# Bringing V back from DRAM by row groups of 32 partitions instead of by key blocks

## The chip, the cores and the metric

The kernel runs on one core of one Trainium2 chip. The metric is the device time of one execution in microseconds. The kernel before takes 347.27 us (median of 3 runs, 345.57 to 350.7). The profile that this document reads is one further execution with a time of its own, 347.75 us, whose span from the first to the last instruction is 346.0 us. Engines are named as the profile names them: PE is TensorE, PEld its weight loads, DVE is VectorE, ACT is ScalarE, POOL is GpSimd, SP is SyncE, which here issues nearly all the DMAs.

## The reference, cut to what matters

Two transformer mixers run one after the other on 256 positions of width 1024, each after an RMS norm whose scale, shift and gate come from a conditioning vector c:

```
cond = silu(c)
for i in range(2):
    shift, scale, gate = split(cond @ ada_w[i] + ada_b[i], 3)
    h = rms_norm(x, norm_g[i]) * (1 + scale) + shift
    y = nsa_mixer(h, ...) if i == 0 else moba_mixer(h, ...)
    x = x + gate * y
```

Both mixers project h by a matrix (`w_in`, to q, keys, values and a gate z), normalise and rotate q and k, attend with 16 heads that share 4 key/value heads of 64 channels, multiply by silu(z) and project back (`w_out`). At 256 positions the selection of blocks in both mixers keeps every block that a query may see. So layer 0 (NSA) adds up three attentions: over 15 compressed keys, over all earlier keys, and over a window, with two separate sets of keys and values (`ks, vs` and `kw, vw`). Its compressed keys come from blocks of 32 positions that go through a small network (`cmp_w1`, a GELU, `cmp_w2`). Layer 1 (MoBA) is one causal attention with one set of keys and values.

## The kernel before, in words

Positions lie in two tiles of 128 (m = 0, 1). Weights come from DRAM in pieces of 512 KB into five buffers named `raw` (`plan.tag("raw", ...)`, line 584; the first projection's pieces use twelve buffers `early`). ACT rounds a piece to `hi`, DVE takes the rest to `lo`, and the `raw` buffer is free again once DVE has read it; PE multiplies with `hi` and `lo` in three passes (`product`). Pieces of `cmp_w1` and of the conditioning matrix `ada_w` are multiplied by PE straight from `raw`, and free it when PE has read it.

**V's way through DRAM.** The products of weights and V work on a quarter of the PE array each: `values` (line 1032) multiplies 32 keys by 64 channels in row group a, the partitions 32a to 32a+31. Row group a needs, for every key block b of 32 keys, that block's V on its own partitions. V comes out of the projection with one position on each partition, so it goes through a DRAM scratch tensor, `VD`. `spread` (line 1129) writes V to `VD` in one DMA (`vd<-n_out` in the profile) and reads it back with eight: for each of the two key tiles kt and each of four key blocks b, one DMA brings the 32 rows of block b four times, once to each row group. `spread` is called once in each layer (lines 1244 and 1525). A row of V has 512 elements in layer 0 (two sets of values) and 256 in layer 1. In layer 0, key tile 0 lands in the tensor `X` (whose content is reloaded later) and key tile 1 in the buffer `vr`; in layer 1 both land in `vr`. In layer 0 the compression network stands at the same place of the program: `cmp_steps` (line 1267) has four steps, and step kq multiplies two pieces of `cmp_w1`, one for keys and one for values. Steps 0 and 1 use pieces loaded before the read-backs or beside them, steps 2 and 3 pieces that come after.

**What sets the order.** All code is recorded first. `Plan._order` then plays the recorded steps in a simple model of the engines: whenever an engine is free, it takes the step that can start first, and among equals the one with the lowest number in the table `TURNS` (2333 numbers, one for each step). Each engine executes its steps strictly in the order that results, and so does SP with the DMAs. In the model a DMA's data are seen `LANDED` = 700 ns after its last byte. No instruction's work depends on the model's times; they set the order alone.

Of the kernel before, what the change touches and what calls it, by code (L numbers as in the profile page):

```python
# [18 lines left out]
P = 128  # L19
# [19 lines left out]
BREATH = 3000.0  # L39
TURNS = [  # L40
# [116 lines left out]
ISSUE, FIRST_BYTE, RATE, LANDED = 450.0, 1500.0, 330.0, 700.0  # L157
# [12 lines left out]
class Plan:  # L170
# [101 lines left out]
    def record(self, engine, method, args, kw):  # L272
# [13 lines left out]
        if "dma" in method:  # L286
            op["bytes"] = self.bytes
        if engine == "T":
            op["mode"] = (aps[1].shape[0], aps[1].shape[-1]) if "tile_position" in kw else None
# [1315 lines left out]
```

## Time and profile before

| | |
|---|---|
| median of 3 runs | 347.27 us |
| profiled execution | 347.75 us, span 346.0 us |
| PE busy | 308.0 us, 89% of the span |
| DVE busy | 248.8 us, 72% |
| ACT busy | 198.6 us, 57% |
| POOL busy | 26.3 us, 8% |
| moved by DMA | 70.89 MB, 205 GB/s over the span |
| mean granted PE clock | 0.964 |

In the profile nearly all work carries line 509, the line at which `issue` hands out recorded steps, so tiles are told apart by name. `raw<-in_nsa_cmp_w_dram` is a load of a piece of `cmp_w1`; `vr<-vd` and `X<-vd` are the read-backs of V; `vd<-n_out` is the write of V to DRAM. In a row of the timeline stand the start, the duration, the engine, the operation, the tile written and the tiles read, a count, and in brackets how long the engine stood idle before it and who released it. In a row of the windows stand, for a stretch of the span, its length, the busy time of each engine, the PE clock granted on average, the mean busy share of the 16 DMA engines, and what they moved. A row that SP has is the issuing of a DMA, not its transfer.

### The profile page before, as it was taken

Reading aid. Unit: us, or ns where it says so; the run is one execution under the profiler, and the core shown is the slowest. Engines: PE = TensorE matmul, PEld = TensorE weight load, DVE = VectorE, ACT = ScalarE, POOL = GpSimd, SP = SyncE. Lnnn points to the kernel's source line nnn. Section 1 sums busy time; section 2 is a strip of 40 time slices with the busy share of each in tenths; the row PEclk is TensorE's granted clock in tenths of the full one; section 3 lists DMA queues with packets and bytes.
Section 4 is the critical chain, followed back from the end, with each engine's and each line's share of the span. In section 5 each row is a group of like instructions: output and inputs, shape, how many; then the busy total and the mean of one; then the engine's idle time right before and its main releaser. Section 6 shows DMA issues by size and latency. Waiting matters only on the chain.

```text
span 346.0 us, 7930 instructions
## 1 busy us (share of the span) xinstructions
PE 308.0 (89%) x3147; PEld 246.5 (71%) x3147; DVE 248.8 (72%) x521; ACT 198.6 (57%) x466; POOL 26.3 (8%) x98
## 2 busy tenths in 40 slices
PE   3999999998058799999999999999993799999995
PEld 2866686886025587877678878866782699998874
DVE  3364363796309689887879497897592599999896
ACT  5444153833205487469578694587481389969430
POOL 5000007960000000000000000010000000000000
PEclk9999999999659989999999999999998799999999
DMA  8999995364759925966786617925439364255543
GB/s 249 333 359 357 364 359 164 96 177 139 192 162 312 303 71 184 300 196 221 270 265 227 236 61 221 309 82 160 127 129 294 113 185 121 73 182 178 163 142 121
DMA packets 46688, 70.89 MB, mean 205 GB/s; under 512 B 3914, under 2 KB 21945, under 8 KB 46652
## 3 DMA queue, kind: packets, MB, share of 16 engines
q1 hardware_dynamic: 46484, 70.34, 64.3%
q8 instruction: 24, 0.39, 0.5%
q14 instruction: 12, 0.10, 0.1%
q10 hardware_dynamic: 168, 0.06, 0.1%
HBM read 68.55 MB, written 1.84 MB: 203 GB/s over the span
## 4 chain that ended last, share of the span: by engine, by line
PE 63%; DVE 12%; DMA 11%; ACT 5%; issue 3%; ACTq 0%; DVEq 0%
PE ps L509 38%; PE acc L509 25%; DMA raw<-in_moba_w_in_dram 5%; DMA raw<-in_nsa_cmp_w_dram 4%; DVE lo L509 4%; DVE p L509 2%; ACT hi L509 2%; DMA raw<-in_nsa_w_in_dram 2%; DVE rs L509 2%; DVE n_out L509 1%; ACT p L509 1%; DVE n_in L509 1%; DVE ss L509 1%; ACT n_out L509 0%; ACT n_in L509 0%
## 5 line engine op out<-in xcount | busy, mean ns | idle before, releaser
L509 DVE TENSOR_TENSOR lo<-raw,hi 128x1024 fp32r<-128x1024 f32 (+1 forms) x50 | 58.9, 1188 | 20.1 <-ACT hi L509 20.0
L509 ACT CAST hi<-raw 128x1024 fp32r<-128x1024 f32 (+1 forms) x50 | 50.7, 1025 | 35.2 <-PE acc L509 13.0
L509 PE MATMUL acc<-hi,HT 128*128 128x512 f32 (+1 forms) x176 | 56.7, 395 | 8.2 <-ACT hi L509 8.2
L509 PE MATMUL acc<-HT,hi 128*128 128x256 f32 x256 | 49.6, 288 | 0.0
L509 ACT ACTIVATE p<-ps,tiny 128x128 f32<-128x128 f32 (+1 forms) x96 | 39.4, 425 | 14.6 <-DVE tiny L509 9.1
L509 PEld LDWEIGHTS acc<-hi,HT 128*128 128x128 f32 x176 | 32.7, 193 | 16.4 <-ACT hi L509 9.3
L509 PEld LDWEIGHTS acc<-HT,hi 128*128 128x128 f32 x256 | 40.0, 189 | 2.9 <-issue 2.5
L509 PE MATMUL acc<-HT,lo 128*128 128x256 f32 x128 | 35.8, 285 | 0.0
L509 PE MATMUL acc<-lo,HT 128*128 128x512 f32 (+1 forms) x88 | 33.8, 395 | 1.5 <-DVE lo L509 1.5
L509 PE MATMUL ps<-KTA,qg 128*128 128x256 f32 (+1 forms) x192 | 31.4, 297 | 3.3 <-ACT qg L509 2.0
L509 PEld LDWEIGHTS ps<-KTA,qg 128*128 128x128 f32 x192 | 26.9, 197 | 7.3 <-ACT qg L509 2.1
L509 DVE TENSOR_REDUCE tiny<-ps 128x2 f32<-128x512 f32 (+2 forms) x40 | 24.8, 630 | 9.7 <-PE ps L509 8.6
L509 PE MATMUL ps<-hi,HT 128*128 128x512 f32 (+1 forms) x96 | 27.1, 362 | 0.0
L509 PEld LDWEIGHTS acc<-HT,lo 128*128 128x128 f32 x128 | 23.9, 189 | 1.2 <-DVE lo L509 0.8
L509 PE MATMUL ps<-hi,qg 128*128 128x256 f32 (+1 forms) x96 | 22.9, 320 | 0.0
L509 PE MATMUL acc<-hi,qg 128*128 128x512 f32 x64 | 21.2, 400 | 0.9 <-DVE zT L509 0.9
L509 DVE STREAM_TRANSPOSE p<-p 128x1536 f32<-128x1536 f32 x12 | 21.2, 1770 | 1.0 <-ACT p L509 1.0
L509 ACT ACTIVATE p<-p,tiny 128x256 f32<-128x256 f32 x48 | 21.1, 501 | 1.3 <-DVE tiny L509 1.1
L509 PE MATMUL ps<-raw,p 128*64 128x256 f32 x64 | 10.4, 447 | 12.4 <-issue 7.9
L509 PEld LDWEIGHTS acc<-lo,HT 128*128 128x128 f32 x88 | 16.8, 193 | 6.0 <-DVE lo L509 3.4
L509 PEld LDWEIGHTS ps<-hi,HT 128*128 128x128 f32 x96 | 16.9, 188 | 4.7 <-issue 2.3
L509 ACT ACTIVATION_READ_ACCUMULATOR p<-ps,tiny 128x1 f32 x96 | 20.1, 209 | 0.0
(197 smaller groups left out, 565.0 us busy)
## 6 DMA issues: line engine op xcount, KB each, us to landing
raw<-in_ada_w_dram SPq DMA_DIRECT2D x32, 512.0 KB
raw<-in_moba_w_in_dram SPq DMA_DIRECT2D x20, 512.0 KB
early<-in_ada_w_dram SPq DMA_DIRECT2D x16, 512.0 KB
early<-in_nsa_w_in_dram SPq DMA_DIRECT2D x12, 512.0 KB
raw<-in_nsa_w_in_dram SPq DMA_DIRECT2D x12, 512.0 KB
raw<-in_nsa_cmp_w_dram SPq DMA_DIRECT2D x8, 512.0 KB
raw<-in_nsa_w_out_dram SPq DMA_DIRECT2D x8, 512.0 KB
raw<-in_moba_w_out_dram SPq DMA_DIRECT2D x8, 512.0 KB
```

The source lines that it names most:

```text
L509: getattr(self.engines[op["engine"]], method)(*[self._real(a) for a in args], **{k: self._real(a) for k, a in kw.items()})
```

## The change

The eight read-backs of a layer are cut the other way. One DMA now belongs to a row group a and a key tile: it writes the 32 partitions of that group, and each partition receives four rows of V, one from each key block, side by side. Bytes, rows and row lengths are the same as before: eight DMAs of 256 KB in layer 0 and eight of 128 KB in layer 1. What differs is the shape of each: before, the source was walked as 4 (the same block again) x 32 rows and the destination was 128 partitions with one row each; now the source is 32 x 4 rows and the destination 32 partitions with four rows each.

In the planner's model, a DMA that writes to DRAM is now seen 2500 ns after its last byte (`WRITTEN`), where it was 700 ns. The table `TURNS` is another one throughout.

```
+WRITTEN = 2500.0
 TURNS = [
-    43, 50, 44, 32, 67, 40, 45, 47, 48, 68, 2321, 2326, 51, 60, 2301, 92, 2330, 2329, 2331, 2332, 41, 81, 63, 54, 77,
...
+    53, 14, 13, 51, 47, 2296, 45, 54, 46, 15, 10, 12, 2292, 22, 2286, 2287, 2328, 2327, 2330, 2331, 69, 59, 60, 16, 31,
...
         if "dma" in method:
             op["bytes"] = self.bytes
+            op["landed"] = WRITTEN if str(args[0].space).endswith("DRAM") else LANDED
...
                 wire = max(wire, start + ISSUE + FIRST_BYTE) + op["bytes"] / RATE
-                seen = wire + LANDED
+                seen = wire + op["landed"]
...
         for kt, dst in enumerate(parts):
-            for b in range(4):
-                at = bass.AP(tensor=VD[l].tensor, offset=VD[l].offset + (kt * P + 32 * b) * n, ap=[[0, 4], [n, 32], [1, n]])
-                Q.dma_start(dst[:, b], at, touches=(dst[:, b], VD[l]))
+            for a in range(4):
+                to = dst[32 * a:32 * a + 32]
+                at = bass.AP(tensor=VD[l].tensor, offset=VD[l].offset + kt * P * n, ap=[[n, 32], [32 * n, 4], [1, n]])
+                Q.dma_start(to, at, touches=(to, VD[l]))
```

The new order is close to the old one on each engine except in the first projection, where PE takes the products of the pieces in another sequence. Three places matter below. The first is SP's queue in layer 0, from the last of the first six read-backs to the first piece of the next projection. Before:

```order
L509 DMA X_69<-vd0_131 128x1x512
L509 DMA raw_0_544<-in_nsa_cmp_w1_dram 128x4x256
L509 DMA vr_0_808<-vd0_131 128x1x512
L509 DMA raw_3_668<-in_nsa_cmp_w1_dram 128x4x256
L509 DMA raw_4_674<-in_nsa_cmp_w1_dram 128x4x256
L509 DMA raw_1_568<-in_nsa_cmp_w1_dram 128x4x256
L509 DMA raw_2_604<-in_nsa_w_in_dram 128x2x512
```

Now, where the first row stands for two read-backs:

```order
L511 DMA X_69<-vd0_131 32x4x512 x2
L511 DMA raw_0_571<-in_nsa_cmp_w1_dram 128x4x256
L511 DMA raw_3_686<-in_nsa_cmp_w1_dram 128x4x256
L511 DMA raw_4_704<-in_nsa_cmp_w1_dram 128x4x256
L511 DMA raw_1_587<-in_nsa_cmp_w1_dram 128x4x256
L511 DMA raw_2_627<-in_nsa_w_in_dram 128x2x512
```

Six read-backs stand ahead of the four pieces for steps 2 and 3 in both; a seventh stood between these pieces before and now comes later, after five more loads of the next stage, and the eighth comes later still.

The second place is PE's queue at step 2 of the compression. `ps<-identF,y` are the transposes that make the keys of layer 0 (four in a row), `acc<-..HT` the last products of the stage before, and `ps<-raw,p` the compression's products. Before:

```order
L509 MATMUL acc_0_283<-lo_0_228,HT_126 128x304
L509 MATMUL acc_0_283<-hi_3_322,HT_126 128x304
L509 MATMUL ps_2_182<-identF_71,y_0_146 128x128 x4
L509 MATMUL ps_3_203<-identF_71,y_1_346 128x128 x4
L509 MATMUL ps_5_230<-identF_71,y_0_146 128x128 x4
L509 MATMUL ps_1_177<-raw_0_544,p_1_742 64x256
L509 MATMUL ps_1_177<-raw_3_668,p_0_740 64x256
```

Now:

```order
L511 MATMUL acc_0_283<-lo_2_319,HT_126 128x304
L511 MATMUL acc_0_283<-hi_3_322,HT_126 128x304
L511 MATMUL ps_1_165<-identF_71,y_0_146 128x128 x4
L511 MATMUL ps_5_230<-identF_71,y_1_361 128x128 x4
L511 MATMUL ps_3_203<-raw_0_571,p_1_752 64x256
L511 MATMUL ps_3_203<-raw_3_686,p_0_747 64x256
```

The third group of transposes has moved from ahead of step 2 to behind it; the rest is as before, in other buffers.

The third place is SP's queue in layer 1, from the write of V on; `raw<-in_moba_w_in` are pieces of layer 1's projection. Before:

```order
L509 DMA vd1_132<-n_out_1_253 128x2x256
L509 DMA raw_3_668<-in_moba_w_in_dram 128x2x512
L509 DMA raw_0_544<-in_moba_w_in_dram 128x2x512
L509 DMA vr_0_808<-vd1_132 128x1x256 x8
L509 DMA raw_4_674<-in_moba_w_in_dram 128x2x512
```

Now:

```order
L511 DMA vd1_132<-n_out_1_253 128x2x256
L511 DMA raw_1_587<-in_moba_w_in_dram 128x2x512
L511 DMA raw_2_627<-in_moba_w_in_dram 128x2x512
L511 DMA vr_0_811<-vd1_132 32x4x256 x5
L511 DMA raw_0_571<-in_moba_w_in_dram 128x2x512
L511 DMA vr_0_811<-vd1_132 32x4x256
L511 DMA raw_1_587<-in_moba_w_in_dram 128x2x512
```

Five read-backs, not eight, now stand ahead of the next piece; one follows it, and two come after four more pieces.

226 rows, old and new, of the table TURNS are left out of this document.

## The prediction

> **What bounds the kernel now.** I read the page's slices first, then windows around the places where PE is not full, the chain that ended last, and SP's and PE's timelines there. In the page's 40 slices (8.65 us each) PE is full except at the start and the end and at two holes:
>
> ```profile
> PE   3999999998058799999999999999993799999995
> PEclk9999999999659989999999999999998799999999
> ```
>
> The holes are the slices from 86.5 us and from 259.5 us, and in both PEclk falls: the clock follows the idling. The chain names what ended them:
>
> ```profile
> 85.36 13.62 DMA raw<-in_nsa_cmp_w_dram
> 258.83 10.06 DMA raw<-in_moba_w_in_dram
> ```
>
> Both are waits for weight pieces, the first for the compression's, the second for layer 1's projection. The windows say what the DMA engines did meanwhile:
>
> ```profile
> core 0: us, PE busy (x) PEld busy (x) DVE busy (x) ACT busy (x) POOL busy (x), PEclk, DMA share, GB/s
> 74.00:83.00 9.00, 7.60 (x59) 6.67 (x58) 8.64 (x26) 0.61 (x2) 1.22 (x4) 1.00 0.29 107
> 104.00:110.00 6.00, 5.12 (x28) 3.20 (x24) 5.79 (x15) 3.10 (x4) 0.00 (x0) 1.00 0.99 346
> 247.00:252.00 5.00, 5.00 (x24) 4.08 (x23) 4.31 (x15) 2.37 (x5) 0.00 (x0) 1.00 0.85 255
> 252.00:259.00 7.00, 7.00 (x32) 5.77 (x31) 7.00 (x11) 5.88 (x7) 0.00 (x0) 1.00 0.28 95
> 123.00:260.00 137.00, 133.68 (x1647) 106.77 (x1647) 111.28 (x228) 97.45 (x254) 0.96 (x1) 1.00 0.59 190
> ```
>
> With weight pieces in flight (104 to 110 us) the engines are 99% busy and move 346 GB/s. While V comes back (74 to 83 and 252 to 259 us) 28 or 29% of them are busy and move 95 to 107 GB/s: between four and five of 16. Four is the outermost count of these transfers' source. Between the holes PE is busy for 133.68 of 137 us at full clock, so what is gained at the first hole stays gained: everything behind it follows PE.
>
> **First hole: 14.5 us if the read-backs use all engines.** SP's and PE's rows (a raw load's row covers the issue of the x pieces):
>
> ```profile
> 68.47 2.45 SPq L509 DMA_DIRECT2D raw<-in_nsa_cmp_w_dram  x2
> 71.43 0.64 SPq L509 DMA_DIRECT2D vr<-vd  x1
> 77.21 2.50 SPq L509 DMA_DIRECT2D X<-vd  x1
> 79.81 2.51 SPq L509 DMA_DIRECT2D raw<-in_nsa_cmp_w_dram  x1
> 85.36 7.94 SPq L509 DMA_DIRECT2D raw<-in_nsa_cmp_w_dram  x3
> 78.78 3.74 PE L509 MATMUL ps<-raw,p 128*64 128x256 f32 x32 [0.92 <-DVE p L509]
> 84.38 1.18 PE L509 MATMUL ps<-identF,y 128*128 128x128 f32 x8 [0.28 <-ACT y L509]
> 99.03 3.66 PE L509 MATMUL ps<-raw,p 128*64 128x256 f32 x14 [3.59 <-DMA raw<-in_nsa_cmp_w_dram]
> 103.20 1.95 PE L509 MATMUL ps<-raw,p 128*64 128x256 f32 x16
> ```
>
> Steps 0 and 1 of the compression run from 78.78 to 82.52 us; step 2 waits until 99.03 for its second piece, and step 3 ends at 103.20 + 1.95 = 105.15. The late read-backs take SP 2.5 us each to issue: 256 KB at 107 GB/s are 2.45 us, so SP is held to the four engines' pace, and the pieces behind it start late as well.
>
> Now the same with all engines. Up to 71.43 what differs is the order within the first projection (below) and one 48-column load that stands three rows later in SP's queue; PE multiplies three other pieces ahead of its use, so I cost it at nothing, or a microsecond if that cover is gone. The first read-back starts as before, and the engines are free of the two pieces ahead at about 74. Six read-backs are 1.57 MB: 4.5 us at 346 GB/s, to 78.5. Step 2's first piece (0.52 MB, 1.5 us) follows, to 80.0. Its second piece needs the buffer that step 0 frees, half way through PE's first row at 80.65. From issue to use I take 4.7 us, from a piece on full engines:
>
> ```profile
> 102.72 3.36 SPq L509 DMA_DIRECT2D raw<-in_nsa_w_in_dram  x3
> 107.43 1.05 ACT L509 CAST hi<-raw 128x1024 fp32r<-128x1024 f32 x1 [1.86 <-DMA raw<-in_nsa_w_in_dram]
> ```
>
> (102.72 to 107.43). That gives 85.4; step 3's last piece, whose buffer is free at 82.52, comes at 87.2. PE has transposed until 85.56. So step 2 runs to 87.5 (1.95 us at full clock), the two groups of transposes to 88.7, step 3 to 90.7. Against 105.15 this is 14.5 us, and DVE and ACT work that waited behind it moves along. What is late next is the projection's pieces. Their buffers are freed by steps 1 to 3, and DMA in the stage is the cap:
>
> ```profile
> 74.00:119.30 45.30, 28.88 (x176) 19.77 (x174) 25.87 (x66) 13.66 (x24) 1.22 (x4) 0.85 0.70 211
> ```
>
> 45.3 us at 211 GB/s are 9.56 MB. At 346 GB/s they take 27.6 us, to 101.6; the stage would end at 119.3 - 14.5 = 104.8. It fits, with 3.2 us to spare.
>
> **Do 32 partitions use all engines?** No read-back of that shape is in the trace. Small loads are:
>
> ```profile
> rot<-in_c_dram ACTq DMA_DIRECT2D x1, 4.0 KB
> y<-in_norm_g_dram ACTq DMA_DIRECT2D x1, 8.0 KB
> y<-in_ada_b_dram ACTq DMA_DIRECT2D x1, 24.0 KB
> y<-in_nsa_cmp_b_dram ACTq DMA_DIRECT2D x1, 2.0 KB
> y<-in_nsa_cmp_pe_dram ACTq DMA_DIRECT2D x1, 16.0 KB
> q10 hardware_dynamic: 168, 0.06, 0.1%
> ```
>
> In rows of 512 B these are 8, 16, 48, 4 and 32 rows, 108 packets. The queue shows 168, 60 more, which is 8 + 16 + 16 + 4 + 16: one more packet for each engine if a transfer uses the largest count up to 16 that divides its rows. The 32-row load then used 16; with 4 the sum would be 156. The Trainium skill, DMA: Bandwidth & Descriptors, section on why a DMA increments its semaphore by 16, states both this count and one completion write per engine.
>
> The rate of such a transfer is unknown. Upper bound: 346 GB/s. Lower, short of no change: half of it, 173. Against the change speaks the Trainium skill's SBUF page (SBUF — State Buffer), section Door 1, the DMA port swizzle: 32 neighbouring partitions reach 8 of 16 ports, measured at 189 GB/s against 328 for 128 partitions; no transfer here shows it, and its ratio would put the time about 2 us over the upper bound's. At half rate the six read-backs end at 83.1, four pieces at 1.5 us each follow to 89.1 and step 3 ends at 91.1, 0.4 us later; but the stage's 1.83 MB of read-backs (seven) take 5.3 us more, to 106.9, which is past 104.8 by 2.1. So the first hole gives 14.5 or 12.4 us. I take the middle, 13.5.
>
> **Second hole: 9.0 us.**
>
> ```profile
> 248.97 8.38 SPq L509 DMA_DIRECT2D vr<-vd  x8
> 257.44 20.10 SPq L509 DMA_DIRECT2D raw<-in_moba_w_in_dram  x7
> 259.99 1.27 ACT L509 CAST KTA<-ps 128x512 fp32r<-128x512 f32 x2 [0.23 <-PE ps L509]
> 268.98 1.04 ACT L509 CAST hi<-raw 128x1024 fp32r<-128x1024 f32 x1 [7.72 <-DMA raw<-in_moba_w_in_dram]
> 262.09 0.39 PE L509 MATMUL acc<-hi,HT 128*128 128x512 f32 x1
> 270.07 1.22 PE L509 MATMUL acc<-hi,HT 128*128 128x512 f32 x2 [7.60 <-ACT hi L509]
> 270.00:280.00 10.00, 9.93 (x55) 8.79 (x56) 8.19 (x15) 5.20 (x9) 0.00 (x0) 0.84 0.39 115
> ```
>
> SP needs 8.38 us for eight read-backs; the piece behind them is issued at 257.44 and used at 268.98, while PE has run dry at 262.48. Now five read-backs (0.66 MB) go ahead of the piece. The engines are free of the two pieces before at about 252, so they end at 253.9 (half rate 255.8), and the piece with 1.5 us and a landing of some 0.7 us at 256.1 (258.0). ACT, free at 261.3 after its KTA casts, rounds it by 262.4: PE waits 0 to 0.4 us. The hole of 7.60 shrinks by 7.4 in both cases; the pieces behind take 1.5 us of DMA each, under what PE spends on one. With the hole goes the slow clock behind it: 0.84 over 10 us is 1.6 us. Together 9.0.
>
> **The other edits.** The later `WRITTEN` only enters the order. The read-backs pushed back are used by the products of attention weights and V, which begin here in the two layers:
>
> ```profile
> L509 PEld LDWEIGHTS ps<-p,vr x736: 127/131/133, 144.5 to 325.3; 32*64 32x64 f32 x184
> 293.65 1.70 PE ps L509 x71
> ```
>
> The last read-backs land 20 us and more ahead of 144.5 and 293.65, also with both shifts, so they cost nothing. The table's other moves (first projection, attention) carry the same instructions, and I cost them at zero, with 3 us either way: PE's idle time outside the holes is 38 - 12 - 7.6 = 18 us, and an order can add or save a part of that.
>
> ```profile
> 80.00:90.00 10.00, 5.93 (x46) 4.70 (x42) 7.19 (x18) 4.98 (x10) 0.00 (x0) 0.94 0.51 142
> 90.00:100.00 10.00, 2.06 (x8) 0.89 (x10) 0.01 (x1) 0.00 (x0) 0.00 (x0) 0.50 0.85 226
> PE 308.0 (89%) x3147; PEld 246.5 (71%) x3147; DVE 248.8 (72%) x521; ACT 198.6 (57%) x466; POOL 26.3 (8%) x98
> ```
>
> (38 is 346.0 - 308.0; 12 is 20 - 5.93 - 2.06, all of it of the first hole.)
>
> **Sum.** Against the profiled 347.75 us: 13.5 + 9.0 = 22.5, so 325.3; at the bounds 324.3 and 326.3. The median of the runs shown, 347.27, is 0.5 lower; I forecast 325.
>
> **The rivals.**
>
> *The order gives a part back.* One hole closes and another opens: the stage up to 119 us has 3.2 us of DMA to spare at best, and DVE, which frees most `raw` buffers, is nearly as loaded as PE there. For it: the table is wholly new. Against: the rows of SP and PE around the holes hardly move. If the first hole gives half, 6.8 us, the time is 347.75 - 6.8 - 9.0 = 332.
>
> *The rate stays.* If the new shape again moves 107 GB/s, only the order helps: one read-back fewer ahead of steps 2 and 3 (2.45 us) and three of 131 KB fewer at the second hole (4.1 us at 95 GB/s): 341. Against: the count of packets above.
>
> *Nothing gained.* The new order eats those 6.5 us: 347.
>
> *Slower: the read-backs now block every engine.* Before, they held four engines; now each one stands ahead of the pieces on all 16. If 32 partitions accept rows much slower than the four engines delivered, the pieces come later than before. The point where that decides: step 3 starts at 103.2 as before if 74 + 1.57 MB / rate + 6.0 + 0.7 = 103.2, a rate of 70 GB/s. At 50 the six take 31.4 us and the first hole grows by 9 us; at the second the five take 13.1, the piece lands at 267.3 and 1.7 us are still gained: 355. Against: four engines alone deliver 107 GB/s with the same rows.
>
> **How the numbers follow.** Forecast 0.70 (319 to 331: the bounds 324.3 and 326.3, the order's 3 us, and 2 more below if PE's idle time at 110 to 119 goes too). Part given back 0.11 (331 to 338). Rate stays 0.09 (338 to 344). Nothing 0.05, slower 0.05. The range 319 to 337 holds about 0.8. Two per cent, about what a measurement of this kernel can tell from no change, is 340.3: faster is 0.70 + 0.11 + 0.04 = 0.85, same 0.05 + 0.05 = 0.10, slower 0.05.
>
> **What would show it.** Right: read-backs with a DMA share over 0.8 and a rate of 170 GB/s or more; SP issuing them in under 1 us each; step 3 ending near 91 us; no gap over 1 us on PE near 250 and a PE clock of 1.00 there. Wrong: a DMA share near 0.28 during the read-backs (the rate stayed), a share near 1 at under 100 GB/s (ports), or the holes gone and new waits of PE elsewhere (the order).

## The result and the profile after

The changed kernel takes 324.2 us (median of 4 runs, 323.95 to 324.33) against 346.99 us (median of 4 runs of the kernel before): the ratio is 0.933, with a 95% interval of 0.925 to 0.940. Here and below a median is over all runs of a kernel, while a ratio leaves out, on both sides, runs more than 1.5% above the fastest of their kernel. Its profiled execution took 324.33 us, with a span of 322.2 us; that of the kernel before took 347.75 us, with 346.0. All lines below carry line 511 where the kernel before had 509.

The page of the changed kernel, with busy times and, in slices of 8.06 us each, the share that PE is busy and the granted clock, shows neither hole, and the clock stays up but for one slice (7, from 169 us):

```profile
PE 302.4 (94%) x3147; PEld 244.8 (76%) x3147; DVE 247.4 (77%) x521; ACT 197.9 (61%) x466; POOL 27.4 (9%) x98
PE   2999999998889999999998999999998999999995
PEclk9999999999999999999997999999999999999999
```

PE has the same 3147 instructions. Its busy time fell by 5.6 us (308.0 to 302.4) and its idle time by 18.2 us (38.0 to 19.8): the waits went, and with them most of the slow clock (mean granted clock 0.964 before, 0.995 now).

The windows of the changed kernel (length, busy time of PE, PEld, DVE, ACT and POOL, clock, DMA share, GB/s) show the read-backs of layer 0, the weight pieces behind them, and the read-backs of layer 1:

```profile
74.00:79.00 5.00, 3.90 (x30) 3.38 (x31) 4.74 (x16) 0.61 (x2) 0.00 (x0) 1.00 1.07 231
79.00:82.00 3.00, 3.00 (x27) 2.58 (x24) 2.97 (x7) 0.00 (x0) 0.00 (x0) 1.00 1.12 215
82.00:86.00 4.00, 2.68 (x19) 2.01 (x17) 1.38 (x4) 3.64 (x8) 0.00 (x0) 1.00 1.08 339
235.00:239.00 4.00, 4.00 (x19) 3.30 (x18) 4.00 (x6) 3.29 (x5) 0.00 (x0) 1.00 1.12 235
```

The DMA share went from 0.28 or 0.29 to 1.07 and more, the rate from 95 to 107 GB/s to 215 to 235. It did not go to 346: all engines are busy, but they move less than when weight pieces have them alone (339 from 82 us on). SP's and PE's timelines show what that does to the first hole:

```profile
69.92 0.96 SPq L511 DMA_DIRECT2D vr<-vd  x2
70.93 0.43 SPq L511 DMA_DIRECT2D X<-vd  x1
71.40 0.51 SPq L511 DMA_DIRECT2D vr<-vd  x1
71.95 1.58 SPq L511 DMA_DIRECT2D X<-vd  x2
75.35 6.28 SPq L511 DMA_DIRECT2D raw<-in_nsa_cmp_w_dram  x4
77.56 3.74 PE L511 MATMUL ps<-raw,p 128*64 128x256 f32 x32 [0.39 <-DVE p L511]
86.14 1.94 PE L511 MATMUL ps<-raw,p 128*64 128x256 f32 x14 [0.84 <-DMA raw<-in_nsa_cmp_w_dram]
89.04 1.96 PE L511 MATMUL ps<-raw,p 128*64 128x256 f32 x16
```

SP issues six read-backs in 3.6 us (69.92 to 73.53), where the late ones of the kernel before took 2.5 us each. PE's wait for step 2's piece is 0.84 us, and step 3 ends at 89.04 + 1.96 = 91.00 us instead of 105.15. In layer 1 PE's longest wait near the old hole is this one, where 7.60 us stood:

```profile
246.11 0.66 PE L511 MATMUL ps<-identF,y 128*128 128x128 f32 x4 [0.90 <-ACT y L511]
```

Places of the program that both orders have show where the 23.8 us of span went. First the kernel before, then the changed one: the first attention product of layer 0, the transposes at the start of layer 1, and the transposes ahead of its attention.

```profile
119.34 1.02 PE L509 MATMUL ps<-KTA,qg 128*128 128x256 f32 x4 [1.97 <-ACT qg L509]
227.08 0.84 PE L509 MATMUL ps<-identF,n_in 128*128 128x128 f32 x4 [0.32 <-ACT n_in L509]
280.54 0.70 PE L509 MATMUL ps<-identR,n_parts 128*128 128x128 f32 x6
```

```profile
103.72 0.50 PE L511 MATMUL ps<-KTA,qg 128*128 128x256 f32 x2 [0.34 <-ACT qg L511]
210.62 0.83 PE L511 MATMUL ps<-identF,n_in 128*128 128x128 f32 x4 [0.29 <-ACT n_in L511]
256.34 0.89 PE L511 MATMUL ps<-identR,n_parts 128*128 128x128 f32 x8 [0.62 <-DVE n_parts L511]
```

| stretch | gained in it, us | from |
|---|---|---|
| up to step 0 of the compression | 1.2 | 78.78 - 77.56 |
| steps 0 to 3 | 12.9 | (105.15 - 91.00) - 1.2 |
| the rest of the stage | 1.5 | (119.34 - 103.72) - 14.15 |
| layer 0's attention and output | 0.8 | (227.08 - 210.62) - 15.62 |
| layer 1's projection, with the second hole | 7.7 | (280.54 - 256.34) - 16.46 |
| layer 1's attention to the end | -0.4 | 23.8 - 24.2 |

The first row is no more than scatter: the runs below start step 0 between 77.06 and 78.85 us, whichever read-backs come after it.

### The profile page after: what moved, and what is told of

Same layout as the page of the kernel before. It is cut to its first block, busy times and chain, and to the rows that moved or that the text cites. A ratio compares the mean times of both kernels' runs of the same rounds, so it can differ in the third digit from the quotient of the medians.

```text
span 322.2 us, 7934 instructions
## 1 busy us (share of the span) xinstructions
PE 302.4 (94%) x3147; PEld 244.8 (76%) x3147; DVE 247.4 (77%) x521; ACT 197.9 (61%) x466; POOL 27.4 (9%) x98
## 4 chain that ended last, share of the span: by engine, by line
PE 67%; DVE 12%; DMA 9%; ACT 4%; issue 2%; ACTq 0%; DVEq 0%
PE ps L511 41%; PE acc L511 26%; DVE lo L511 4%; DMA raw<-in_moba_w_in_dram 3%; ACT hi L511 2%; DMA raw<-in_ada_w_dram 2%; DMA raw<-in_nsa_cmp_w_dram 2%; DMA raw<-in_nsa_w_in_dram 2%; DVE p L511 2%; DVE rs L511 2%; DVE tiny L511 1%; DVE n_out L511 1%; DVE ss L511 1%; ACT p L511 1%; DVE KTA L511 0%
## 5 line engine op out<-in xcount | busy, mean ns | idle before, releaser
L511 PE MATMUL acc<-hi,HT 128*128 128x512 f32 (+1 forms) x176 | 56.0, 388 | 1.1 <-ACT hi L511 1.1
L511 PE MATMUL acc<-HT,hi 128*128 128x256 f32 x256 | 51.5, 292 | 0.0
L511 PEld LDWEIGHTS acc<-HT,hi 128*128 128x128 f32 x256 | 41.0, 193 | 2.3 <-issue 1.9
L511 PE MATMUL acc<-HT,lo 128*128 128x256 f32 x128 | 37.0, 292 | 0.0
L511 PE MATMUL ps<-KTA,qg 128*128 128x256 f32 (+1 forms) x192 | 30.7, 294 | 0.3 <-ACT qg L511 0.3
L511 PEld LDWEIGHTS ps<-KTA,qg 128*128 128x128 f32 x192 | 26.1, 193 | 4.0 <-issue 1.1
L511 PEld LDWEIGHTS acc<-HT,lo 128*128 128x128 f32 x128 | 24.7, 194 | 2.3 <-issue 1.9
L511 DVE TENSOR_TENSOR lo<-early,hi 128x1024 fp32r<-128x1024 f32 (+1 forms) x17 | 17.3, 1032 | 1.3 <-ACT hi L511 1.0
```

Of the source, the lines that this page charges most:

```text
L511: getattr(self.engines[op["engine"]], method)(*[self._real(a) for a in args], **{k: self._real(a) for k, a in kw.items()})
```

## The experiments

Which part of the change does it, how the two layers share it, what sets the new rate, and whether it can be raised: these were the questions, in this order. The times are medians, with the ratio to runs of the kernel before on the same chip.

### The new shape alone, the old order

```
         for kt, dst in enumerate(parts):
-            for b in range(4):
-                ... ap=[[0, 4], [n, 32], [1, n]]
+            for a in range(4):
+                ... ap=[[n, 32], [32 * n, 4], [1, n]]
```

in the kernel before, with its own `TURNS` and 700 ns.

> The kernel before with its own table of turns and its own 700 ns, where only the read-backs are cut by row groups. Theory (the rate is what counts, both holes were the four engines' slowness): the six read-backs move over 200 GB/s, and step 3 of the compression ends at 91 to 92 us, as in the changed kernel, with at most 1 us for the seventh read-back that stands between the pieces of steps 2 and 3; in layer 1 eight read-backs (1.05 MB) at 215 GB/s take 4.9 us and let the piece behind them in at about 257 to 259 us of the old clock, before ACT is free at 261.3, so the second hole is under 1 us. Time 324 to 327 us. Rival (the new table of turns closes the holes, the rate does little): step 3 ends at 100 us or later and the time is 341 us or more. In between: 0.5 to 4 us over the changed kernel would be the share of the table.

Measured: 327.17 us (326.45 to 327.26), ratio 0.940 (0.935 to 0.945). The shape by itself gives nearly all of the gain. The changed kernel is 3.0 us faster still, but the intervals of the two ratios overlap, so that the new order adds something here is likely and not shown. One number was missed: step 3 ends 3.6 us or more later than expected, at 93.65 + 1.95 = 95.60 us. The timelines of SP and PE, a window and a row of the chain of this run, and the same row of the changed kernel:

```profile
77.00 0.30 SPq L509 DMA_DIRECT2D vr<-vd  x1
79.11 3.21 SPq L509 DMA_DIRECT2D raw<-in_nsa_cmp_w_dram  x3
89.45 3.68 PE L509 MATMUL ps<-raw,p 128*64 128x256 f32 x14 [1.16 <-DMA raw<-in_nsa_cmp_w_dram]
93.65 1.95 PE L509 MATMUL ps<-raw,p 128*64 128x256 f32 x16
82.00:86.00 4.00, 2.21 (x15) 1.39 (x13) 1.43 (x4) 4.00 (x9) 0.00 (x0) 1.00 1.11 199
79.11 10.30 DMA raw<-in_nsa_cmp_w_dram
```

```profile
79.61 6.49 DMA raw<-in_nsa_cmp_w_dram
```

The seventh read-back stands between the pieces here, so from 82 to 86 us the engines are still at 199 GB/s with a share of 1.11, where the changed kernel already moves 339. The pieces in the queue crawl with the read-back: step 2's second piece, issued at 79.11 us, lands after 10.30 us, in the changed kernel after 6.49. These 3.8 us are more than the read-back's own bytes (0.26 MB, 1.2 us at 215 GB/s). The clock adds to it: behind the longer wait step 2's products take 3.68 us (89.45), in the changed kernel 1.94 (86.14).

### The new order alone, the old shape

The edit is the reverse: the changed kernel with the old loop over b.

> The changed kernel with its new table and its 2500 ns, but with the read-backs cut by key block as before. Theory: the rate stays at 95 to 110 GB/s with 28% of the DMA engines busy, and the table gains only the one read-back fewer ahead of steps 2 and 3 (2.45 us) and three of 131 KB fewer at the second hole (4.1 us): 341 us, 339 to 343. Rival (the table alone closes the holes): 324 to 330 us. Second rival (the table by itself gains nothing, or loses): 346 us or more.

Measured: 342.92 us (339.07 to 346.07), ratio 0.982 (0.974 to 0.990), inside the 339 to 343 expected. A window of layer 0 and PE's row at the second hole, of this run, with a row of SP and one of the chain:

```profile
75.00:80.00 5.00, 3.90 (x31) 3.42 (x31) 4.75 (x15) 0.61 (x2) 0.00 (x0) 1.00 0.28 103
264.04 1.12 PE L511 MATMUL ps<-identF,y 128*128 128x128 f32 x4 [6.49 <-ACT y L511]
250.04 0.62 SPq L511 DMA_DIRECT2D vr<-vd  x1
250.77 11.55 DMA raw<-in_moba_w_in_dram
```

The share is 0.28 again, and both holes are there. The order gains 5.0 us by itself (347.9 to 342.9); by the interval it may be 3.4 to 9, and a gain under 2% is at the edge of what these runs can tell. At the second hole PE still waits 6.49 us, where 4.1 us were to go. The last two rows, of SP and of the chain, say why. The piece that comes late is the one behind the sixth read-back, not the one behind the fifth: it is issued at 250.77 us and lands 11.55 us later.

### The old shape in one layer

```
-        for kt, dst in enumerate(parts):
+        if l == 0:      (in the other run: if l == 1)
+            ... the old loop over b
+        else:
+            ... the new loop over a
```

> The changed kernel with the read-backs of layer 0 alone cut by key block as before; layer 1's stay by row groups. Theory (the first hole is worth 13.5 us, of which the table's one read-back fewer keeps 2.45): 324.2 + 11 = 335 us, 334 to 337, with step 3 of the compression ending at 101 to 103 us and no hole in layer 1. Rival (the first hole's gain came from the table): under 329 us.

> The changed kernel with the read-backs of layer 1 alone cut by key block as before. Theory: the five read-backs ahead of the next piece take 5 x 131 KB / 95 GB/s = 6.9 us in place of 3, so that piece comes about 4 us later, and PE waits for 3 to 5 us of the 9.0 that the second hole was worth, the table having taken the rest: 327 to 329.5 us. Rival (the second hole was not the read-backs', or the table alone closed it): 324 to 325 us. Second rival (the table gives nothing there): 333 us.

Measured: 337.06 us with the old shape in layer 0 (ratio 0.970, 0.964 to 0.976) and 329.86 with it in layer 1 (0.948, 0.943 to 0.953), both a little past the end of what was expected. So in the new order the shape is worth 12.9 us in layer 0 and 5.7 in layer 1. The sum, 18.6, is what both together are worth (342.92 - 324.2 = 18.7): as far as runs that scatter by several us can tell, the holes don't touch each other. With the old shape in layer 0 step 3 ends at 102.98 us, as expected (101 to 103), and layer 1 has no hole. In the second run PE's row at the hole reads

```profile
249.92 1.12 PE L511 MATMUL ps<-identF,y 128*128 128x128 f32 x4 [6.21 <-ACT y L511]
```

against 0.90 us in the changed kernel: 5.3 of the 5.7 us are this one wait, and the expectation, which counted the five read-backs alone, was low for the same reason as above.

### Fewer engines by another walk of the source

```
-                at = ... ap=[[n, 32], [32 * n, 4], [1, n]])
+                at = ... ap=[[8 * n, 4], [n, 8], [32 * n, 4], [1, n]])
```

and `[[4 * n, 8], [n, 4], ...` in a second run.

> The changed kernel, where the 32 rows of the source are walked as 4 times 8, so that the outermost count is 4 again; destination, bytes and order are the changed kernel's. Theory (the outermost count decides how many engines work): 28% of the DMA engines busy and 95 to 110 GB/s during the read-backs, and the time of the run with the order alone, 343 us (340 to 345). Rival (the destination's 32 partitions decide, or the repeat of the same source rows made the old form slow): all engines busy, over 200 GB/s, 324 us. That is also what comes out if the two counts are merged to 32 when the transfer is made.

> The same with the 32 rows walked as 8 times 4. Theory: eight engines; a row of 2 KB took 84 ns on an engine where four engines worked, so eight move 8 x 2048 B / 84 ns = 195 GB/s with half of the engines busy, only a little under the 215 to 230 GB/s that all sixteen move now: 324 to 326.5 us. Rival (a row takes 150 ns whenever the destination has 32 partitions): 110 GB/s and 340 us or more. If the two counts are merged: all engines busy and 324 us.

Measured: 326.18 us (323.61 to 327.6) and 322.26 us (322.06 to 327.05), and in both all engines were busy:

```profile
75.00:79.00 4.00, 3.17 (x24) 2.91 (x26) 3.78 (x14) 0.61 (x2) 0.00 (x0) 1.00 1.06 234
75.00:79.00 4.00, 2.91 (x21) 2.41 (x21) 3.77 (x12) 0.37 (x1) 0.00 (x0) 1.00 1.07 216
```

This is what was expected for merged counts, since 4 steps of 8n and 8 steps of n are one walk of 32 steps of n. So the runs did not confine the transfer, and whether a count of 4 that can't be merged uses four engines without the zero step of the old walk stays untried. What they do give is two more measurements of what look like the same transfers: their medians lie 4 us apart. The granted clock moves along: of the runs of these two kernels, those granted 0.99 had spans of 324.3 to 325.8 us, those granted 1.00 319.7 to 320.3, and the three between (0.995 to 0.998) 320.4 to 323.4.

### All ports: other partitions, the same bytes

In one run each read-back writes all 128 partitions from 128 rows; in the other it writes every fourth partition with the source unchanged.

```
+            for b in range(4):
+                at = ... ap=[[n, P], [1, n]])
+                Q.dma_start(dst[:, b], at, ...)
```

```
-                Q.dma_start(to, at, touches=(to, VD[l]))
+                Q.dma_start(dst[a::4], at, touches=(to, VD[l]))
```

> The changed kernel, where each read-back writes all 128 partitions, each with its own position's row, from a source of 128 rows: bytes, row lengths, number and order of the transfers stay. It leaves out the regrouping of V by key blocks, so the products of weights and V work on other rows. Theory (the 32 partitions of a group can take only 215 to 230 GB/s, as the Trainium skill's page SBUF - State Buffer, section Door 1, the DMA port swizzle, has it for the ports that they reach): rows of 2 KB take 84 to 95 ns, not 150, and the read-backs move 320 to 350 GB/s; step 2's second piece lands some 2 us sooner, and PE loses 1 to 1.5 us less: 322.5 to 323.5 us. Rival (the DRAM side, four reads of the same rows, sets the rate): 215 to 230 GB/s and 324.2 us.

> The changed kernel, where each read-back still writes 32 partitions with four rows each, but every fourth partition of the 128 rather than 32 neighbours; source, bytes, number and order stay. It puts V's rows on other partitions than the products expect, so it leaves the regrouping out. Theory (which partitions, not how many, set the rate; by the Trainium skill's page SBUF - State Buffer, section Door 1, every fourth partition reaches all ports): 320 to 350 GB/s and the time of the run in which each partition takes its own row, 322.5 to 323.5 us. Rival (32 partitions with four rows each are slow wherever they lie): 215 to 230 GB/s, 324.2 us.

Measured: 318.39 us (316.61 to 319.63), ratio 0.914 (0.908 to 0.919), and 318.13 us (316.39 to 322.85), ratio 0.912 (0.906 to 0.918). Windows of the first and of the second run during the read-backs:

```profile
75.00:77.00 2.00, 1.29 (x10) 1.13 (x9) 1.88 (x5) 0.00 (x0) 0.00 (x0) 1.00 1.03 383
74.00:77.00 3.00, 2.30 (x17) 2.05 (x16) 2.83 (x8) 0.00 (x0) 0.00 (x0) 1.00 1.02 388
```

At the same share the rate is 383 and 388 GB/s, not 215 to 235. The second run has the same source, the same 32 partitions for a transfer and the same four rows on each as the changed kernel; only their places differ. So where the 32 partitions lie sets the rate. The Trainium skill, SBUF — State Buffer, section Door 1, the DMA port swizzle, gives 189 GB/s for partitions 0 to 31, 328 for all 128 (at 1 MiB), and 218 as the limit of the eight ports; the rates here, 206 to 235 GB/s, lie around that limit and up to 8% above it, not at 189, and the ratio agrees (0.58 there; 231 / 388 = 0.60 here).

Share and rate also give, as an estimate, how long one row of 2 KB holds an engine: 0.28 x 16 x 2048 B / 103 GB/s = 89 ns with the old shape (the run with the order alone), 1.07 x 16 x 2048 B / 231 GB/s = 152 ns in the changed kernel, 1.02 x 16 x 2048 B / 388 GB/s = 86 ns on every fourth partition. So the rows of the old shape, repeated from the same source, were as quick as any; what it lacked was engines.

The time was missed: 5.8 us under the changed kernel, where 0.7 to 1.7 were expected. The landmarks of the first run:

```profile
102.05 0.47 PE L511 MATMUL ps<-KTA,qg 128*128 128x256 f32 x2
206.38 0.84 PE L511 MATMUL ps<-identF,n_in 128*128 128x128 f32 x4 [0.20 <-ACT n_in L511]
```

Against 103.72 and 210.62 of the changed kernel, 1.7 us are gained up to the first landmark (2.2 counted from step 0, which starts 0.5 us later in this run); from the second to the end of the span (322.2 and 315.9) 2.1 us more. The 2.6 us between lie in the attention of layer 0, where no read-back is waited for. There a window of the changed kernel has the clock at 0.96, which is 1.6 us in 40, and the same window of this run has it at 1.00:

```profile
140.00:180.00 40.00, 39.15 (x686) 30.93 (x685) 29.95 (x55) 28.30 (x95) 0.00 (x0) 0.96 0.73 253
```

```profile
140.00:180.00 40.00, 39.52 (x706) 31.83 (x705) 30.48 (x56) 29.90 (x101) 0.00 (x0) 1.00 0.73 243
```

So the slow rate of 32 neighbours costs the changed kernel 3.8 us in waits, and some 2 us come with the clock. The mean clock was 0.994 to 0.998 in three of the changed kernel's four runs and 0.999 to 1.000 in all four of this one. That the slow rows bring the dip is not shown, and one trace speaks against it: the profiled run on every fourth partition has the fast rows, PE waits for no piece there at step 2, and still its clock dips in layer 0 (mean clock 0.988, 322.85 us):

```profile
100.00:140.00 40.00, 38.23 (x467) 30.61 (x465) 31.73 (x79) 25.61 (x73) 0.00 (x0) 0.91 0.67 218
```

At a clock of 1.000 the changed kernel's span is 320.4 us in the one run that had it, and this one's 314.9 to 317.9 in three, which fits the 3.8 us.

### Both halves of the partitions at once

By the Trainium skill, SBUF — State Buffer, section Door 1, the DMA port swizzle, groups 0 and 1 lie behind other ports than groups 2 and 3. So the read-backs of the latter were issued from a second queue, POOL's or ACT's; a third run deals the groups out so that three of the first six are on each side.

```
+                Q.dma_start(to, at, touches=(to, VD[l]),
+                            on="G" if a > 1 else None)      ("A" in the second and third run)
-            for a in range(4):
+            for a in ([0, 1, 2, 3], [2, 3, 0, 1])[kt]:      (third run alone)
```

> The changed kernel, where the read-backs of row groups 2 and 3 are issued by POOL, those of groups 0 and 1 stay on SP; everything else is in the changed kernel's order. POOL has nothing else to do after 71.2 us. Theory (each row group takes rows at 215 to 230 GB/s because of where its partitions lie; groups 0, 1 and groups 2, 3 lie behind different ports, as the Trainium skill's page SBUF - State Buffer, section Door 1, the DMA port swizzle, has it): with both halves under way at once the rows take 84 to 110 ns and the read-backs move 280 GB/s or more, step 2 of the compression does not wait, and the time comes near that of the two runs on all ports: 318 to 321 us. Rival (the engines' rate for this source, or all 32-partition writes together, sets it): 215 to 230 GB/s as now, 324 us. Second rival (POOL's issuing is slow, several us for each, and the late rows hold up the pieces): 326 us or more.

> The same with groups 2 and 3 issued by ACT. Theory: the same rate as with POOL, and ACT, idle for 3.9 us before 77.2 us, has room for it in layer 0; in layer 1, where ACT is busy for 3.3 of 4 us, the four issues of some 0.4 us and their wait for V's write to DRAM push the rounding of weight pieces back by up to 2 us, of which PE feels a part: 319 to 323 us, at or above the time with POOL. Rival: 324 us, no gain from two queues.

> The run with two queues on ACT, with the row groups dealt out anew, so that three of layer 0's first six read-backs (groups 0 and 1) are on SP and three (groups 2 and 3) on ACT; before, it was two and four, and the two had left SP's queue before ACT's began to move, so that nothing ran side by side. Theory (groups 0, 1 and groups 2, 3 are held up apart from each other): while both queues have rows under way, from about 74.7 to 77 us, rows of 2 KB take 84 to 110 ns and 280 GB/s or more are moved; the six end 1.5 to 2 us sooner than with one queue, and the time is 320 to 322 us. Rival (all 32-partition writes share one limit): rows take 150 to 170 ns there too, 205 to 230 GB/s, and the time is that of the run with two queues on ACT, 323 to 324 us.

Measured: 323.18 us (ratio 0.928, 0.923 to 0.932), 323.71 (0.926, 0.919 to 0.932) and 323.34 (0.920, 0.915 to 0.926): at the changed kernel's 0.933 (0.925 to 0.940) or slightly below, not clearly told apart from it. The six runs of the third kernel take 318.9 to 325.71 us, so its time decides between none of the forecasts. The rate does: it did not rise. A window of the first run, then the third run's window and its two queues in it (packets, MB, share of 16 engines):

```profile
77.00:80.00 3.00, 2.61 (x23) 2.34 (x23) 2.89 (x9) 0.61 (x2) 0.00 (x0) 1.00 1.04 206
```

```profile
78.00:79.50 1.50, 1.38 (x14) 0.94 (x16) 1.44 (x7) 0.39 (x2) 0.00 (x0) 1.00 1.06 220
q10 hardware_dynamic: 102, 0.20, 62.8%
q1 hardware_dynamic: 76, 0.13, 43.1%
```

In the third run both queues moved rows for 1.5 us at 220 GB/s in all. The last of these expectations is wrong in that nothing ran side by side before: in the run on ACT, from 75 to 76 us, 66 packets of SP's queue and 54 of ACT's moved at 215 GB/s, with a share of 1.05. In layer 1 all three runs have such a stretch: 225 GB/s with POOL (236.5 to 239 us), 217 with ACT (233 to 235), 224 in the third run (238 to 239), where the queues' packets also include some rows of weight pieces. In each of these stretches the rival is right: two halves side by side are no faster, and none comes near 280 GB/s. The third run's step 3 ends no sooner either: PE waits 1.48 us for step 2's second piece there. Why the halves do not add up stays open; a limit of each half's own ports alone would let them.

### Fewer bytes

```
+                nb = a + 1 if kt else 4
-                at = ... ap=[[n, 32], [32 * n, 4], [1, n]])
+                at = ... ap=[[n, 32], [32 * n, nb], [1, n]])
-                Q.dma_start(to, at, ...)
+                Q.dma_start(to[:, 0:nb], at, ...)
```

> The changed kernel, where the read-back of key tile 1 for row group a brings the key blocks 0 to a alone, the ones that the products use; the output is whole. Six of 32 row blocks fall away in each layer, 19% of the bytes; 393 KB in layer 0. Theory (the rate through 32 partitions is what still costs): 393 KB at 215 GB/s are 1.8 us less ahead of step 2 at most, and PE's two waits there (0.62 and 0.84 us) shrink or go: 322.5 to 323.7 us. Rival (nothing of it is on the path): 324.2 us.

Measured: 325.49 us (322.69 to 325.64), ratio 0.932 (0.926 to 0.937): the time of the changed kernel, as the rival has it. In PE's timeline and the chain

```profile
77.87 3.74 PE L511 MATMUL ps<-raw,p 128*64 128x256 f32 x32 [0.38 <-DVE p L511]
84.40 0.62 PE L511 MATMUL ps<-raw,p 128*64 128x256 f32 x2
85.84 1.94 PE L511 MATMUL ps<-raw,p 128*64 128x256 f32 x14 [0.82 <-DMA raw<-in_nsa_cmp_w_dram]
88.73 1.95 PE L511 MATMUL ps<-raw,p 128*64 128x256 f32 x16
79.92 5.88 DMA raw<-in_nsa_cmp_w_dram
```

the wait of 0.62 us ahead of step 2 is gone, but the next one is 0.82 us as against 0.84, and step 3 ends at 90.68 instead of 91.00. Counted from step 0, which starts at 77.87 here and at 77.56 in the changed kernel, that is 0.6 us sooner. The last row, of the chain, shows the piece that step 2 waits for: it was issued at 79.92 us, when step 0 had freed its buffer, and landed 5.88 us later, against 6.49 in the changed kernel. So fewer bytes in the queue do bring it 0.6 us sooner after its issue, which is too little for these times to tell, and they cannot bring the issue forward. Of the versions that compute the whole output, none beats the changed kernel by more than its runs scatter.

## Why the prediction was right, point by point

**Time and direction.** 325.0 us was forecast and 324.2 came; against the profiled execution the sum was 22.5 us, and the times differ by 347.75 - 324.33 = 23.4. The mechanism is borne out; that the total comes so close is in part luck, as the terms below show.

**What bounds the kernel.** Right. The read-backs' four engines made both holes: with the shape alone the kernel takes 327.17 us, without it 342.92.

**First hole, 13.5 us.** Right in size. Step 3 was to end between 90.7 and 91.1 us and ended at 91.00. The gain at the first attention product is 15.6 us, of which 1.2 were there before step 0; the runs with the order alone and with the shape alone start step 0 at 78.11 and 77.06 us, and runs in the changed kernel's order between 77.53 and 78.85, so this part is scatter. The read-backs were to end at 78.5 to 83.1 us; they ended near 82, by the change of rate in the windows. The sum at half rate left out the 0.7 us of landing that the others have; with it step 3 would have ended at 91.8.

**32 partitions use 16 engines.** Right: the share is 1.07 in place of 0.28.

**The rate, between 346 and 173 GB/s.** The mis-sized step. The measured 215 to 235 lies between the bounds, nearer to the lower, and so the rule of the Trainium skill's page SBUF — State Buffer was the better guide. The 2 us that the prediction gives for that page's ratio do not follow from its own sum: at 189 / 328 x 346 = 199 GB/s seven read-backs take 9.2 us in place of 5.3, to 105.5, which is 0.7 past 104.8. But the step's price, between 0 and 2.1 us with the middle taken, was too small: with 383 to 388 GB/s the kernel is 5.8 us faster, 3.8 of them in waits. In layer 0 the bound of 2.1 about held (1.7 measured, 2.2 from step 0 on); what was missed lies in layer 1, where the sum had the second hole shrink alike at both rates and the runs show 2.1 us between them.

**Second hole, 9.0 us.** A little too much: 7.7. PE was to wait 0 to 0.4 us there and waits 0.90 for ACT's `y` at 246.11 us and 0.62 ahead of attention. The clock near it is 1.00, as forecast. The 0.7 us of landing in the sum are the planner's `LANDED`; no run measures them by themselves. The 4.1 us that the order was to bring there by itself were 1.1 (7.60 to 6.49), since the sixth read-back was not counted; with the fast shape that costs little.

**The other edits.** Costed at nothing for the read-backs pushed back, and rightly: none of PE's waits in the changed kernel is for a read-back of V. The range's upper end, 331, has 1.7 us more than the terms that it names (326.3 and 3).

**What made up for it.** The sum had left out the slow clock behind the first hole. This window of the kernel before

```profile
119.00:130.00 11.00, 10.66 (x62) 9.40 (x62) 9.08 (x29) 9.75 (x38) 0.00 (x0) 0.84 0.31 110
```

is 11 x (1 - 0.84) = 1.8 us, which the prediction counted for the second hole alone. Of these 1.8 us only 0.8 show in layer 0's attention and output, since the changed kernel has a dip of its own there (0.96 over 40 us). With these 0.8, the earlier step 0 and the rest of the stage (1.2 and 1.5 us, inside the 3 us either way that the other edits were given), the shortfalls cancel. That they cancel so nearly is luck.

**The rivals.** "The order gives a part back": it did not, the changed kernel is 3.0 us faster than the shape alone, though their intervals overlap. "The rate stays", priced at 341: the run that puts just this case to the test took 342.92, so the price of the order, 6.5 us, was 1.5 too high by the medians, which is within the scatter (339.07 to 346.07). "The read-backs block every engine": the effect exists, since the pieces crawl with the read-backs (199 GB/s with one read-back among them), but at 215 GB/s, not below the 70 from which it would have decided.

**What would show it.** All came: a share over 0.8 and over 170 GB/s, read-backs issued in 0.4 to 0.8 us each, step 3 near 91, no wait over 1 us near 250 and a clock of 1.00.

## What to carry to other kernels

Where a DMA's share of the engines is a clean fraction (here 0.28, four engines and a little), look at the outermost count of its walk before its bytes: the same bytes cut the other way were worth 20 us here. A count that merges with the next one into one walk did not confine the transfer. Once all engines are busy, look at the rate beside the share: 1.07 at 231 GB/s against 1.02 at 388 says that each row takes longer, and here the places of the partitions within one transfer decided that, not their number. A slow transfer costs also what stands behind it in the same queue, so its place among other loads is worth a look as well.

## What the runs showed of the hardware that was not expected

Every fourth of 128 partitions takes rows at 388 GB/s where 32 neighbours take 231, with the same source and the same count. Four by eight steps of one uniform walk are spread over the engines like 32 steps. The granted clock moves by 1% between runs of one kernel, and the span by 4 to 6 us with it (319.7 to 320.3 us at 1.00, 324.3 to 325.8 at 0.99). The two kernels whose read-backs ran at 383 and 388 GB/s were granted 0.997 to 1.000 in seven of eight runs and 0.988 in the eighth, so fast rows do not rule a dip out.
